# Two-layer hybrid trunk in split fp32: a new home and an earlier place for the weight sums of the mixers' output product, and an earlier place in DVE's queue for the third operand's split in the block products

## The chip, the cores and the metric

The kernel runs on one core of a Trainium2 chip. The metric is the time of one execution on the device in microseconds (us). The numbers of the time before are the median and the extremes of three runs; one further execution was taken by the hardware profiler, and every row of a view below is from that one. Engines are named as the profile names them: PE (matmul; PEld is its weight load), DVE (vector), ACT (scalar), POOL (GpSimd, here a queue of DMAs), SP (another queue of DMAs).

## The reference, cut to what matters

512 positions of width 1024 go through two layers in float32. Each layer is feed-forward, mixer, feed-forward:

```
for l in range(2):
    x = x + 0.5 * swiglu(rmsnorm(x, ln_ffn1[l]), w_ffn1_gu[l], w_ffn1_down[l])
    h = rmsnorm(x, ln_mix[l])
    u_pool, q, k, v, gate_logits = split(h @ w_in[l])
    a = pool_mixer(u_pool, pool_w[l], pool_scale[l]) @ w_pool_branch[l]
    b = swa_sink_attention(rope(norm(q)), rope(norm(k)), v, sinks[l]) @ w_attn_branch[l]
    g_pool, g_attn = split(sigmoid(gate_logits))
    x = x + (g_pool * a + g_attn * b) @ w_out[l]
    x = x + 0.5 * swiglu(rmsnorm(x, ln_ffn2[l]), w_ffn2_gu[l], w_ffn2_down[l])

swiglu(h, w_gu, w_down): g, u = split(h @ w_gu); return (silu(g) * u) @ w_down     # 1024 -> 2 x 2816 -> 1024
```

## The kernel before, in words

**Split products.** Every float32 operand is written as a rounded high part and a low part (the rest). ACT writes the high part with a cast (`wh<-raw`, `op<-fb`), and DVE writes the low part with a subtraction (`wl<-raw,wh`, `op<-fb,op`). A product is three matmuls: high by high, high by low, low by high.

**Block products.** Most large products are done in seven block products in place of eight, in the order of `ORDER` (line 27): a11, s1, s2, a12, s3, s4, a22. Each name stands for a weight block and an operand block; those of s1 to s4 are sums or differences of others. `strassen` (line 568) runs them. Each block product has two weight tiles, c = 0 and 1, and for each tile two column halves q = 0 and 1. After c = 0 it calls `W.prep()`, and after c = 1 the step of that block (`steps[kind]`, which takes the result out of PSUM) and then `W.prep()` again. Work that other engines are to do beside the matmuls hangs in the table `mid`: an entry `(kind, c, q)` is called when those matmuls have been written, so it stands in each engine's queue at that point. Results sit in three PSUM accumulators: a11, s2, s3 and a22 share one (A), s1 and s4 one (C), a12 has the third (D). A block that starts on an accumulator waits until the last result has been taken out of it.

**One queue for each engine.** The class `Engines` keeps every engine's instructions in the order in which the program writes them. An instruction that waits holds up all that stands behind it on its engine.

**The weights' pipeline** (class `Weights`, lines 184 to 326). `plan` lists all weight tiles in order of use. `load` brings tiles from HBM into 7 buffers (`raw`). SP issues the load, and where a block is a sum of two matrices, POOL issues a second DMA that adds the other matrix into the same buffer. A buffer is free once its `uses` are 0. `prep` keeps the high parts 4 tiles ahead of PE and the low parts 3 tiles ahead. The weights of s2 and s4 are sums of tiles that are there already; `add_up` writes them with DVE (`sums<-raw`) into `W.sums`. While `W.sums` is `None`, `add_up` stops at the first such tile, and the raw tiles that go into it keep their use.

**Feed-forward** (`ffn`, line 603). The 2816 hidden columns are worked in column groups, 512 or 384 wide at a time (`block`), and after two such blocks `down` (line 810) multiplies them by the down weights with a block product of its own. Each feed-forward has three downs: one with 384 columns (weight tiles of 1024 and 512 columns) and two with 512. The last one (`final`) is followed by the next norm, whose operands are already made beside it: `feeds` (line 558) writes PE transposes of x at fixed places of s3, s4 and a22, some into accumulator D. In `down` the operand of s3 is `f["b"]`; `high("s3", ...)` is called at `("s2", 0, 1)`, `low("s3")` in the step `s2`, after the `add` that takes the result of s2 into x. A block's result goes to two places of x in most cases: one by DVE (`add`), the other by an ACT copy into a buffer (`aside`) and a DMA on POOL that adds the copy into x (`gathered`).

**Mixer** (`mix`, line 922). After q, k, v, u and the gates, the loop over m (line 1241) runs eight branch products with the weights `br`, whose operands include the tiles `ah` and `al`; the last one, m = 7, writes into the PSUM tile `sc`. The output product with `w_out` follows as a block product. Its operand blocks are quarters of `ze`, made by DVE (`less`), and their split parts live in three places: `place[0]` for a11, a12 and a22, `place[1]` for s1 and s3, `place[2]` for s2 and s4. The first two operands are split in the loop itself (`beside`, at m = 4 to 7). `W.sums` is given its buffers after the loop, in the home of `al`. The step of a11 copies the result into `aside[0]` (`copied(0, ...)`, profile name `zo<-mm`), `gathered(0, 0, 0)` at `("s1", 1, 0)` adds it into x (`x<-zo` on POOL), and the step of s2 copies into the same `aside[0]` again, so that copy waits for the DMA.

Of the kernel before, what the change touches and what calls it, by code (L numbers as in the profile page):

```python
# [10 lines left out]
F32 = mybir.dt.float32  # L11
F32R = mybir.dt.float32r
# [7 lines left out]
P = 128  # L20
L = 2
S = 512
D = 1024
KT = D // P
FF = 2816
HT = S // 2
# [14 lines left out]
CH = 1024  # L41
# [78 lines left out]
def trunk(ctx, tc, x0, xT, consts, vecs, rows, w_g4, w_g3, w_d8, w_d6, w_qkv, w_u, w_pool, w_gate, w_br, w_out, out):  # L120
# [3 lines left out]
    wh_, wl_, xl = pool("wh", HI, side="left"), pool("wl", LO, side="left"), pool("xl", 1, side="left")  # L124
# [203 lines left out]
    W = Weights()  # L328
# [274 lines left out]
    def ffn(ctx, nm, nxt, last):  # L603
# [3 lines left out]
        sums = ctx.enter_context(tc.tile_pool(name="sums", bufs=2, reuse_waits="tile"))  # L607
# [14 lines left out]
        f, ops, turns = {}, {}, []  # L622
# [65 lines left out]
        def high(name, src, n):  # L688

            ops[name] = op.tile([P, 2, 2, S], F32R, name="op", tag=f"op{AT[name]}")  # L690
            hi, lo = (ops[name][:, i, :, :n] for i in range(2))
            nc.scalar.copy(out=hi, in_=src)
            ops[name, "low"] = lambda: nc.vector.tensor_tensor(
                out=lo, in0=src, in1=hi.bitcast(F32), op=ALU.subtract
            )

        def low(name):
            ops.pop((name, "low"))()
# [111 lines left out]
        def down(n, final):  # L810
# [3 lines left out]
            def add(t, d, c):  # L814
                def go(pt):
                    y = x[:, 2 * t:2 * t + 2, d * S:(d + 1) * S]
                    nc.vector.scalar_tensor_tensor(out=y, in0=pt, scalar=c, in1=y, op0=ALU.mult, op1=ALU.add)
                return go
# [13 lines left out]
            def aside():  # L832
                t, d, c, pt, half = pend_x[0]
                nc.scalar.activation(out=half, in_=pt, func=AF.Copy, scale=c)
# [14 lines left out]

            def s2(pt):  # L850
                add(1, 0, 0.5)(pt)
                low("s3")

            def a12(pt):
                add(0, 0, 0.5)(pt)
# [13 lines left out]
            def a22(pt):  # L869
# [7 lines left out]
            mid = {  # L877
                ("a11", 1, 0): lambda: low("s2"), ("s1", 0, 0): aside, ("s1", 0, 1): lambda: [low("a12"), gathered()],
                ("s2", 0, 1): lambda: [high("s3", f["b"], n), aside()],
                ("s2", 1, 0): gathered, ("a12", 0, 1): lambda: high("s4", f["c"], n),  # L880
                ("s3", 0, 0): lambda: ops.pop("t4")(), ("s3", 1, 0): lambda: high("a22", f["a"], n),
                ("s4", 0, 0): lambda: low("a22"),
            }
# [38 lines left out]
    def mix(ctx, l, nm, nxt):  # L922
        ap = ctx.enter_context(tc.tile_pool(name="ap", bufs=1, reuse_waits="tile"))
        ah, al = (ap.tile([P, 4, S], F32R, name=n) for n in ("ah", "al"))
        rp = ctx.enter_context(tc.tile_pool(name="rp", bufs=1, reuse_waits="tile"))
        mp = ctx.enter_context(tc.tile_pool(name="mp", bufs=1, reuse_waits="tile"))
# [4 lines left out]
        for i in range(3):  # L931
            n = order_.index(i)
# [20 lines left out]
        qkv = mp.tile([P, 5, S], F32, name="qkv")  # L953
# [261 lines left out]
        a, b, c, d = y[0][0], y[0][1], y[1][1], y[1][0]  # L1215
        place, ops = [None] * 3, {}

        def high(name, src):
            t = ops[name] = place[AT[name]]
            hi, lo = (t[:, :, i, :] for i in range(2))  # L1220
            nc.scalar.copy(out=hi, in_=src)
            ops[name, "low"] = lambda: nc.vector.tensor_tensor(
                out=lo, in0=src, in1=hi.bitcast(F32), op=ALU.subtract
            )

        def low(name):
            ops.pop((name, "low"))()
# [13 lines left out]
        for m in range(KT):  # L1241
            w = W.take("br")
            pts = (mm(), mm()) if m + 1 < KT else (wide[:, 0, :], wide[:, 1, :])
            for i, acts in enumerate((
                [part_of(k, slice(0, S)) for k in range(4)], [(ah[:, k, :], al[:, k, :]) for k in range(4)]
            )):
                gemm(pts[i], pairs(w, acts, 4 * i))
            zm = z[2 * m:2 * m + 2]
            for i in range(2):
                nc.scalar.activation(out=zm[i], in_=zm[i], func=AF.Sigmoid)  # L1250
            if m == 4:
                place[0] = rp.tile([P, 4, 2, HT], F32R, name="op0", tag="zo0")
                place[1] = mp.tile([P, 4, 2, HT], F32R, name="op1", tag="qkv")
            if m in beside:
                beside[m]()
            for i in range(2):
                nc.vector.tensor_tensor(out=zm[i], in0=pts[i], in1=zm[i], op=ALU.mult)
            nc.vector.tensor_tensor(out=zm[0], in0=zm[0], in1=zm[1], op=ALU.add)
            W.prep()
# [2 lines left out]
        three = [pf.tile([P, 2, S], F32, name=f"mm{i}") for i in range(3)]  # L1262
        turn = pf.tile([P, 2, S], F32, name="pt")
        roles = [three[i] for i in order_]
        place[2] = ap.tile([P, 4, 2, HT], F32R, name="op2", tag="ah")
        pair = ap.tile([P, 2, CH], F32, name="sums", tag="al")
        W.sums = Parts([pair[:, i, :] for i in range(2)])
        aside = [zo[1][:, 2 * i:2 * i + 2, :] for i in range(2)]

        def region(t, d):  # L1270
# [14 lines left out]
        def gathered(i, t, d):  # L1285
            return lambda: nc.gpsimd.dma_start(out=region(t, d), in_=aside[i], accum_op=ALU.add)
# [8 lines left out]

        def s2(pt):
            copied(0, pt, 1.0)
            low("s3")

        def a12(pt):  # L1300
            add(0, 0, pt)
# [12 lines left out]
        def a22(pt):  # L1314
# [8 lines left out]
        high("s2", a)  # L1323
        mid = {
            ("a11", 1, 0): lambda: low("s2"),
            ("s1", 0, 1): lambda: low("a12"), ("s1", 1, 0): gathered(0, 0, 0), ("s2", 1, 0): gathered(1, 1, 1),
            ("a12", 0, 0): gathered(0, 1, 0),
            ("a12", 0, 1): lambda: high("s4", c), ("s3", 0, 0): lambda: less(a, a, d, -1.0),
            ("s3", 1, 0): lambda: high("a22", a), ("s4", 0, 0): lambda: low("a22"),
# [126 lines left out]
```

## Time and profile before

| what | value |
|---|---|
| median of three runs (lowest, highest) | 1857.6 us (1857.4, 1858.55) |
| the profiled execution's own time | 1857.56 us |
| its span, first to last instruction | 1855.8 us |
| busy share of the span: PE, PEld, DVE, ACT, POOL | 99%, 83%, 78%, 57%, 9% |
| granted PE clock | 1.0 throughout |
| HBM read, mean over the span | 160 GB/s |
| costliest groups: `wl<-raw,wh` on DVE, `wh<-raw` on ACT | 509.3 us, 438.4 us |

A row of the timeline has the start, the time, the engine, the line (always L97, since a helper records everything), the operation, output and inputs by name, and how many were merged; in square brackets stands the idle time of that engine just before it, and what ended that. An end on PE is modelled: matmuls overlap, and one that follows another starts about 0.23 us after it although each is shown with 0.39 us. Idle time in brackets is counted from the modelled end, so the distance between two starts, less 0.23 us, says how much was really lost. A DVE or ACT row shows a little more than the distance between two starts as well (1.22 us for a 128x1024 subtraction, of which one can start every 1.14 us).

### The profile page before, as it was taken

To read this page: it belongs to the slowest core of one execution; us is meant where nothing else is said; L and a number is where in the kernel's file an instruction comes from. 1 tells how busy PE (TensorE), PEld (TensorE's weight loads), DVE (VectorE), ACT (ScalarE), POOL (GpSimd) and SP (SyncE) were. 2 spreads that over 40 slices of the span, in tenths; PEclk is the share of its full clock that TensorE was granted. 3 is DMA by queue.
4 is the path that set the end of the run, shared out by engine and by line. 5 is a ranking of instruction groups with operands and counts; after the bars stand their busy time and mean duration, and the time that the engine had idled before them with its cause. 6 is when DMAs were issued, how large, how long until landed. Compare 5 with 4: busy or idle time off the path is not lost.

```text
span 1855.8 us, 24041 instructions
## 1 busy us (share of the span) xinstructions
PE 1840.7 (99%) x8880; PEld 1548.0 (83%) x8880; DVE 1452.7 (78%) x1825; ACT 1051.4 (57%) x1533; POOL 165.7 (9%) x190
## 2 busy tenths in 40 slices
PE   9999999999999999999999999999999999999999
PEld 9988888887787889988878898888877878899887
DVE  8878878677568987887898878786675689788877
ACT  6655555645447655555675555565554477546554
POOL 0110101000001011110100111110000011101000
PEclk9999999999999999999999999999999999999999
DMA  8877867422247667787767768773222378777864
GB/s 255 210 227 193 216 170 192 132 80 71 82 109 192 193 180 186 191 223 192 195 169 205 169 182 232 199 186 108 91 69 83 100 193 216 178 187 179 244 182 125
DMA packets 97462, 314.85 MB, mean 170 GB/s; under 512 B 10528, under 2 KB 10784, under 8 KB 97344
## 3 DMA queue, kind: packets, MB, share of 16 engines
q1 hardware_dynamic: 67680, 225.57, 35.8%
q0 software_dynamic: 29520, 87.71, 27.5%
q8 instruction: 70, 1.15, 0.2%
q14 instruction: 48, 0.39, 0.1%
q10 hardware_dynamic: 144, 0.03, 0.0%
HBM read 295.44 MB, written 2.10 MB: 160 GB/s over the span
## 4 chain that ended last, share of the span: by engine, by line
PE 84%; DVE 7%; ACT 6%; DMA 2%; issue 1%; POOL 0%; DVEq 0%; ACTq 0%; POOLq 0%; SPq 0%
PE mm L97 76%; PE sc L97 3%; PE pt L97 3%; ACT wh L97 2%; DVE wl L97 2%; DVE sums L97 1%; DVE x L97 1%; DMA x<-zo 1%; ACT sq L97 1%; PE pt_pv L97 1%; ACT xg L97 1%; ACT more L97 0%; DVE more L97 0%; PE pt_tp L97 0%; ACT xgh L97 0%
## 5 line engine op out<-in xcount | busy, mean ns | idle before, releaser
L97 ACT CAST wh<-raw 128x1024 fp32r<-128x1024 f32 (+3 forms) x447 | 438.4, 989 | 285.4 <-PE mm L97 156.4
L97 DVE TENSOR_TENSOR wl<-raw,wh 128x1024 fp32r<-128x1024 f32 (+3 forms) x447 | 509.3, 1146 | 97.3 <-PE mm L97 59.6
L97 PE MATMUL mm<-wh,op 128*128 128x512 f32 x1456 | 464.2, 394 | 0.4 <-ACT zo L97 0.4
L97 PE MATMUL mm<-wh,more 128*128 128x512 f32 (+1 forms) x1104 | 334.0, 373 | 0.0
L97 PEld LDWEIGHTS mm<-wh,op 128*128 128x128 f32 x1456 | 273.2, 188 | 57.6 <-DVE op L97 1.6
L97 PE MATMUL mm<-wh,xgh 128*128 128x512 f32 (+2 forms) x840 | 312.5, 372 | 0.9 <-ACT xg L97 0.8
L97 PE MATMUL mm<-wh,xgl 128*128 128x512 f32 (+2 forms) x840 | 309.5, 368 | 0.0
L97 PE MATMUL mm<-wl,xgh 128*128 128x512 f32 (+2 forms) x840 | 309.4, 368 | 0.0
L97 PE MATMUL mm<-wl,op 128*128 128x512 f32 x728 | 284.0, 390 | 1.6 <-DVE wl L97 1.6
L97 PEld LDWEIGHTS mm<-wh,more 128*128 128x128 f32 x1104 | 205.2, 188 | 29.8
L97 PE MATMUL mm<-wl,more 128*128 128x512 f32 (+1 forms) x552 | 205.9, 373 | 1.2 <-DVE wl L97 1.2
L97 DVE TENSOR_TENSOR wl<-sums,wh 128x1024 fp32r<-128x1024 f32 (+2 forms) x148 | 168.7, 1140 | 44.7 <-ACT wh L97 29.4
L97 ACT CAST wh<-sums 128x1024 fp32r<-128x1024 f32 (+2 forms) x148 | 144.1, 984 | 86.8 <-DVE sums L97 43.7
L97 PEld LDWEIGHTS mm<-wh,xgh 128*128 128x128 f32 x840 | 157.9, 188 | 23.2 <-ACT xg L97 2.1
L97 PEld LDWEIGHTS mm<-wh,xgl 128*128 128x128 f32 x840 | 157.9, 188 | 21.5
L97 PEld LDWEIGHTS mm<-wl,xgh 128*128 128x128 f32 x840 | 158.1, 188 | 21.0 <-DVE wl L97 0.3
L97 PEld LDWEIGHTS mm<-wl,op 128*128 128x128 f32 x728 | 136.9, 188 | 30.1 <-DVE wl L97 3.3
L97 POOL DMA_DIRECT2D raw<-in_w_g x92 | 78.6, 855 | 717.5 <-DMA raw<-in_w_g 266.0
L97 PE MATMUL mm<-xgh,wh 128*128 128x512 f32 x320 | 129.2, 404 | 0.0
L97 PE MATMUL mm<-xgl,wh 128*128 128x512 f32 x320 | 125.3, 391 | 0.5 <-DVE xgl L97 0.5
L97 PE MATMUL mm<-xgh,wl 128*128 128x512 f32 x320 | 125.2, 391 | 0.0
L97 PEld LDWEIGHTS mm<-wl,more 128*128 128x128 f32 x552 | 103.6, 188 | 17.2 <-DVE wl L97 2.4
(252 smaller groups left out, 2252.8 us busy)
## 6 DMA issues: line engine op xcount, KB each, us to landing
raw<-in_w_g SPq DMA_DIRECT2D x160, 512.0 KB, 5.2
raw<-in_w_d SPq DMA_DIRECT2D x100, 512.0 KB, 4.4
raw<-in_w_g POOLq DMA_DIRECT2D x64, 512.0 KB, 6.1
raw<-in_w_g SPq DMA_DIRECT2D x77, 384.0 KB, 4.8
raw<-in_w_d POOLq DMA_DIRECT2D x40, 512.0 KB, 5.7
raw<-in_w_gate SPq DMA_DIRECT2D x32, 512.0 KB, 3.3
raw<-in_w_g POOLq DMA_DIRECT2D x28, 384.0 KB, 6.1
raw<-in_w_out SPq DMA_DIRECT2D x20, 512.0 KB, 3.6
```

What stands on the lines that cost most here:

```text
L97: return lambda *args, **kw: self.tc.keep_in_program_order(call(*args, **kw))
```

## The change

Four things are done. (1) In the loop over m, at m = 4, `W.sums` is opened, in the home of q, k and v, whose tile is no longer read then; `prep` can thus add up the weights of s2 within the loop. (2) The operand of s1 moves from that home to the home of the norm's low part (`xgl`), also no longer read. (3) After the loop, `place[1]` (now for s3 alone) and `place[2]` take the homes of `al` and `ah`. (4) In `down` and in the mixer's output product, `low("s3")` moves from the step `s2` to the entry `("s2", 1, 0)` of `mid`, that is, from behind the taking out of s2's result to half a weight tile before the end of s2's matmuls. What is computed stays the same, and no engine's count of instructions changes.

```
             def s2(pt):
                 add(1, 0, 0.5)(pt)
-                low("s3")
...
-                ("s2", 1, 0): gathered, ("a12", 0, 1): lambda: high("s4", f["c"], n),
+                ("s2", 1, 0): lambda: [low("s3"), gathered()], ("a12", 0, 1): lambda: high("s4", f["c"], n),
...
             if m == 4:
                 place[0] = rp.tile([P, 4, 2, HT], F32R, name="op0", tag="zo0")
-                place[1] = mp.tile([P, 4, 2, HT], F32R, name="op1", tag="qkv")
+                one = xl.tile([P, KT * S], F32R, name="op1", tag="xgl")[:, :2 * CH]
+                place[1] = one.rearrange("p (k i t) -> p k i t", i=2, t=HT)
+                four = mp.tile([P, 5, S], F32, name="sums", tag="qkv")[:, :4, :]
+                W.sums = Parts([four[:, 2 * i:2 * i + 2, :].rearrange("p i t -> p (i t)") for i in range(2)])
...
-        place[2] = ap.tile([P, 4, 2, HT], F32R, name="op2", tag="ah")
-        pair = ap.tile([P, 2, CH], F32, name="sums", tag="al")
-        W.sums = Parts([pair[:, i, :] for i in range(2)])
+        place[1:] = [ap.tile([P, 4, 2, HT], F32R, name=n, tag=n) for n in ("al", "ah")]
...
         def s2(pt):
             copied(0, pt, 1.0)
-            low("s3")
...
-            ("s1", 0, 1): lambda: low("a12"), ("s1", 1, 0): gathered(0, 0, 0), ("s2", 1, 0): gathered(1, 1, 1),
+            ("s1", 0, 1): lambda: low("a12"), ("s1", 1, 0): gathered(0, 0, 0), ("s2", 1, 0): lambda: [low("s3"), gathered(1, 1, 1)()],
```

How this moves the instructions is seen at three places. The first is DVE's queue in the down with 384 columns, around the end of s2; `op<-fb,op` is the low part of s3's operand, `x<-mm` takes out the result of s2, and `wl` and `sums` are weight tiles.

```order
 L97 TENSOR_TENSOR wl<-raw,wh 128x1024
 L97 TENSOR_TENSOR wl<-raw,wh 128x512
+L97 TENSOR_TENSOR op<-fb,op 128x2x384
 L97 SCALAR_TENSOR_TENSOR x<-mm_136,x 128x2x512
-L97 TENSOR_TENSOR op<-fb,op 128x2x384
 L97 TENSOR_TENSOR wl<-raw,wh 128x1024
 L97 TENSOR_TENSOR sums<-sums,raw 128x1024
```

The subtraction stands ahead of the taking out in place of behind it; nothing else moves, and the downs with 512 columns show the same.

The second is DVE's queue at the end of the mixer's loop (the first layer's), before the change. The rows begin at the end of m = 6: `op_4607` is the low part of s1's operand, the rows with `sc` take out m = 7, the `ze<-ze` after them makes the operand of s2, `op_4730` is its low part, and `sums<-raw` the two weight sums of s2.

```order
L97 TENSOR_TENSOR wl<-raw,wh 128x1024
L97 TENSOR_TENSOR op_4607<-ze,op_4607 128x4x256
L97 TENSOR_TENSOR ze<-sc,ze 128x512
L97 TENSOR_TENSOR zo_2993<-sc,zo_2993 128x512
L97 TENSOR_TENSOR ze<-ze,zo_2993 128x512
L97 TENSOR_TENSOR wl<-raw,wh 128x1024
L97 SCALAR_TENSOR_TENSOR ze<-ze 128x4x256
L97 TENSOR_TENSOR wl<-raw,wh 128x1024
L97 TENSOR_TENSOR sums<-raw 128x1024 x2
L97 TENSOR_TENSOR op_4730<-ze,op_4730 128x4x256
L97 TENSOR_TENSOR wl<-sums,wh 128x1024
```

And the same place in the changed kernel, where `ah` is now the name of the home of s2's operand:

```order
L97 TENSOR_TENSOR wl<-raw,wh 128x1024
L97 TENSOR_TENSOR sums<-raw 128x1024 x2
L97 TENSOR_TENSOR op_4607<-ze,op_4607 128x4x256
L97 TENSOR_TENSOR ze<-sc,ze 128x512
L97 TENSOR_TENSOR zo_2993<-sc,zo_2993 128x512
L97 TENSOR_TENSOR ze<-ze,zo_2993 128x512
L97 TENSOR_TENSOR wl<-raw,wh 128x1024
L97 SCALAR_TENSOR_TENSOR ze<-ze 128x4x256
L97 TENSOR_TENSOR wl<-raw,wh 128x1024
L97 TENSOR_TENSOR ah<-ze,ah 128x4x256
L97 TENSOR_TENSOR wl<-sums,wh 128x1024
```

The two sums stand seven instructions earlier, ahead of m = 7's results. ACT's queue has the same order as before here and in the rest of the output product, and so have DVE's later rows.

The third is SP's queue, with the semaphores that each load waits on: the last three loads of `w_out` and the two after them, before the change and then after it. `DMASW7` and `DMASW0` are the adding DMAs on POOL that filled the two tiles of s1, `DMAHW4` and `DMAHW5` the loads that filled those of a11; a load that waits on one of them takes that buffer.

```order
L97 DMA raw<-in_w_out 128x1024 [waits DMASW7_49,DVE_49,Activation_49]
L97 DMA raw<-in_w_out 128x1024 [waits DMAHW4_49,DMAHW2_49]
L97 DMA raw<-in_w_out 128x1024 [waits DMAHW5_49,DMAHW3_49,DVE_49]
L97 DMA raw<-in_w_g 128x1024 [waits DMASW0_49,Activation_49]
L97 DMA raw<-in_w_g 128x1024 [waits DMASW1_49,DVE_49]
```

```order
L97 DMA raw<-in_w_out 128x1024 [waits DMAHW4_49,DVE_49,Activation_49]
L97 DMA raw<-in_w_out 128x1024 [waits DMAHW2_49,DMAHW5_49,DVE_49,Activation_49]
L97 DMA raw<-in_w_out 128x1024 [waits DMASW7_49,DMAHW3_49,DVE_49,Activation_49]
L97 DMA raw<-in_w_g 128x1024 [waits DMASW0_49,DVE_49]
L97 DMA raw<-in_w_g 128x1024 [waits DMASW1_49,DVE_49]
```

The loads keep their order; the buffers they take change. The eighth load of `w_out` takes a buffer of a11 in place of one of s1. The order on POOL is the same in both kernels: the four adding DMAs of `w_out`, then the three `x<-zo`.

## The prediction

> **What bounds the kernel now.** I read the page first, then the waits of PE, then the timeline around each of them.
>
> ```profile
> PE 1840.7 (99%) x8880; PEld 1548.0 (83%) x8880; DVE 1452.7 (78%) x1825; ACT 1051.4 (57%) x1533; POOL 165.7 (9%) x190
> ...
> PE mm L97 <- DVE x L97: 4.0, 7, 1.4
> PE mm L97 <- DVE wl L97: 2.8, 7, 0.4
> PE mm L97 <- ACT xg L97: 0.8, 3, 0.3
> ```
>
> PE runs 99% of the span, so the change can win only what PE loses in waits. The table gives them by their last cause. They are few, and nearly all end with DVE: seven on `x` (a result taken out before PE may transpose x or reuse the accumulator) and seven on `wl` (a low weight part). DVE is busy 78% and is not the bound on average; it is late only where a queue of subtractions stands in front of the one that PE needs. The timeline says where.
>
> In the down with 384 columns (layer 1, second feed-forward; four of these in the program):
>
> ```profile
> 792.42 0.69 DVE L97 TENSOR_TENSOR wl<-raw,wh 128x512 fp32r<-128x512 f32 x1 [1.07 <-ACT u L97]
> 793.95 1.23 DVE L97 SCALAR_TENSOR_TENSOR x<-mm,x 128x1024 f32<-128x1024 f32 x1 [0.84 <-PE mm L97]
> 795.09 0.95 DVE L97 TENSOR_TENSOR op<-fb,op 128x768 fp32r<-128x768 f32 x1
> ...
> 801.44 1.22 DVE L97 TENSOR_TENSOR wl<-sums,wh 128x1024 fp32r<-128x1024 f32 x1
> ...
> 790.44 0.84 ACT L97 CAST op<-fb 128x768 fp32r<-128x768 f32 x1
> ...
> 801.69 0.61 PE L97 MATMUL mm<-wh,op 128*128 128x512 f32 x2
> 802.71 0.50 PE L97 MATMUL mm<-wl,op 128*128 128x512 f32 x1 [0.41 <-DVE wl L97]
> ...
> 806.92 0.39 PE L97 MATMUL mm<-wl,op 128*128 128x512 f32 x1
> 807.31 0.73 PE L97 MATMUL mm<-wh,op 128*128 128x512 f32 x2
> ```
>
> DVE waits 0.84 us for the end of s2, takes its result out (793.95), then splits s3's operand (795.09), and has no idle time from there to 801.44, the low weight for s4. PE wants that at 802.1 and starts at 802.71. Two matmuls take 0.61 us together and one 0.39, so starts are 0.22 to 0.23 us apart. From 801.69 to 802.71 are 1.02 us for two starts: 0.57 lost, and 0.11 more because the first matmul after the wait shows 0.50 us in place of 0.39. At 806.92 to 807.31 another 0.16 goes (a22's low operand, again from DVE's queue), with the same 0.11. That makes 0.95 us per such down.
>
> In the last down of a feed-forward (layer 0, first one; three are followed by a norm):
>
> ```profile
> 313.53 1.23 DVE L97 TENSOR_TENSOR wl<-raw,wh 128x1024 fp32r<-128x1024 f32 x1 [1.50 <-PE mm L97]
> 316.42 1.23 DVE L97 SCALAR_TENSOR_TENSOR x<-mm,x 128x1024 f32<-128x1024 f32 x1 [1.67 <-PE mm L97]
> 317.56 1.22 DVE L97 TENSOR_TENSOR op<-fb,op 128x1024 fp32r<-128x1024 f32 x1
> ...
> 323.24 1.22 DVE L97 SCALAR_TENSOR_TENSOR x<-mm,x 128x1024 f32<-128x1024 f32 x1
> ...
> 311.98 1.04 ACT L97 CAST op<-fb 128x1024 fp32r<-128x1024 f32 x1
> ...
> 337.94 0.63 PE L97 MATMUL mm<-cst,x 128*128 128x128 f32 x4 [0.25 <-DVE x L97]
> ...
> 342.27 0.50 PE L97 MATMUL mm<-xgl,wh 128*128 128x512 f32 x1 [0.23 <-DVE xgl L97]
> ```
>
> The same picture with 1.67 us of idle time before s2's result. Here the backlog reaches x (323.24 is a12's result), the transposes for the next norm (0.25 us idle, which by the rule above is 0.41 lost) and the next stage's first operand (0.23, so 0.39, and 0.11 after it).
>
> In the mixers' output product (layer 0):
>
> ```profile
> 553.83 1.22 DVE L97 TENSOR_TENSOR op<-ze,op 128x1024 fp32r<-128x1024 f32 x1
> 556.80 0.69 DVE L97 TENSOR_TENSOR ze<-sc,ze 128x512 f32<-128x512 f32 x1 [1.75 <-PE sc L97]
> 562.13 2.35 DVE L97 TENSOR_TENSOR sums<-raw 128x1024 f32<-128x1024 f32 x2
> ...
> 573.03 1.22 DVE L97 TENSOR_TENSOR op<-ze,op 128x1024 fp32r<-128x1024 f32 x1
> ...
> 579.77 1.23 DVE L97 TENSOR_TENSOR wl<-raw,wh 128x1024 fp32r<-128x1024 f32 x1 [3.25 <-ACT wh L97]
> ...
> 582.05 1.22 DVE L97 SCALAR_TENSOR_TENSOR x<-mm,x 128x1024 f32<-128x1024 f32 x1
> ...
> 563.46 1.05 ACT L97 CAST wh<-sums 128x1024 fp32r<-128x1024 f32 x1 [1.24 <-DVE sums L97]
> 564.42 1.02 ACT L97 ACTIVATE zo<-mm 128x1024 f32<-128x1024 f32 x1
> ...
> 577.78 1.02 ACT L97 ACTIVATE zo<-mm 128x1024 f32<-128x1024 f32 x1 [3.99 <-DMA x<-zo]
> ...
> 563.41 1.43 SPq L97 DMA_DIRECT2D raw<-in_w_out  x3
> ...
> 567.89 0.84 POOL L97 DMA_DIRECT2D raw<-in_w_out  x1 [20.10 <-DMA raw<-in_w_out]
> 568.43 1.53 POOL L97 DMA_DIRECT2D x<-zo  x1
> 573.41 1.18 POOL L97 DMA_DIRECT2D x<-zo  x1 [3.45 <-ACT zo L97]
> ...
> 578.86 0.50 PE L97 MATMUL mm<-wh,op 128*128 128x512 f32 x1 [0.41 <-ACT zo L97]
> ...
> 583.32 0.66 PE L97 MATMUL mm<-cst,x 128*128 128x128 f32 x4 [1.41 <-DVE x L97]
> ...
> 596.76 0.63 PE L97 MATMUL mm<-cst,x 128*128 128x128 f32 x4 [0.43 <-DVE x L97]
> ...
> 618.84 0.50 PE L97 MATMUL mm<-wh,xgh 128*128 128x512 f32 x1 [0.26 <-ACT xg L97]
> ```
>
> Read backwards: PE waits 1.41 us for a12's result (DVE, 582.05). DVE had stood 3.25 us for an ACT cast behind the copy at 577.78, and that copy had stood 3.99 us for the DMA `x<-zo`, since both use `aside[0]`. The DMA left POOL at 568.43, though its copy was done at 565.4 (564.42 and 1.02): ahead of it POOL stood 20.10 us for the eighth load of `w_out`, which SP issued at 563.41, when the first of the `sums` at 562.13 had freed a buffer. The weight sums thus hold up a DMA of x, and three waits later PE.
>
> **The change part by part.**
>
> *The split of s3 in the down.* One subtraction, with no DMA and no new instruction, moves from behind the taking out to ahead of it. It needs s3's high part, cast by ACT at 790.44 for 0.84 us (done 791.3) and at 311.98 for 1.04 us (done 313.0). DVE is free for it at 793.1 (792.42 and 0.69) and 314.8, so the cast is 1.7 us early. Its cost of 0.95 us falls into 0.84 us of idle time and that of 1.22 us into 1.67. What stood behind it comes 0.85 us and 1.14 us earlier. Behind it on DVE stand s2's `x<-mm` and the weights of s3 and a12; nobody new waits. POOL's `gathered` stands after it in program order only, as its own wait is on ACT and PE.
>
> With 384 columns, 801.44 becomes 800.6, its end 801.8, ahead of the 802.1 at which PE wants it; a22's operand is then late by at most 0.1. I take 0.9 us of the 0.95, times four downs: 3.6 us (2.7 if only the first wait goes, 0.68 each; 3.8 at most). With 512 columns and a norm behind, a12's result moves from 323.24 to 322.1. The wait at 337.94 goes (0.41), and the one at 342.27 for most of its 0.50, together with shorter late starts that no idle column marks; the bound is the 1.14 us by which the queue moves. I take 1.0 us, times three: 3.0 us (1.2 to 3.4). The other five downs show no wait and give nothing.
>
> *The sums of s2 in the mixer.* Two subtract-like additions, 1.14 us each, move to 553.83, ahead of s1's low operand, which then ends at 557.4, and s1 starts on PE near 562. The idle 1.75 us before 556.80 takes most of them; 0.5 us runs over and delays s2's operand. Its part on ACT starts 0.5 us later, but `wh<-sums` behind it loses its wait of 1.24, so the copy at 564.42 comes 0.8 us earlier and ends at 564.6. The sums now need only loads that landed long before and a home that nobody reads, so no wait is added. The eighth load leaves SP when the first sum is done, near 555, in place of 563.41, its adding DMA on POOL is issued near 560 in place of 567.89, and POOL is idle when the copy ends: `x<-zo` leaves at 564.7, 3.7 us earlier. If it takes as long as now (568.43 to 577.78, 9.3 us) it has landed at 574.0. The copy, the cast and DVE's 579.77 follow 3.8 us earlier, and a12's result is then bound by PE's own end of a12 at 578.5, not 582.05: 3.5 us earlier. That is before PE's transposes need it (581.0).
>
> *The homes.* s1's operand, s3's operand and the sums go to tiles whose last readers ended before; no instruction is added. s3's operand no longer overwrites s1's, which costs and gains nothing here, as its cast waits for `ze`.
>
> What is late next: after a12's result the chain runs DVE, ACT, DVE to the next norm's operands, all of it at most 3.5 us earlier. PE loses there, with 0.16 for each idle time and 0.11 after three of them: 0.41, 1.41, 0.43, 0.26, and one on `wl` of 0.4 from the table, 4.0 us in all. I take 3.4, the shift less a little (2.2, the first two alone; 4.0 at most).
>
> The mixer of layer 1:
>
> ```profile
> 1499.97 1.03 ACT L97 ACTIVATE zo<-mm 128x1024 f32<-128x1024 f32 x1 [2.90 <-DMA x<-zo]
> ...
> 1504.24 1.22 DVE L97 SCALAR_TENSOR_TENSOR x<-mm,x 128x1024 f32<-128x1024 f32 x1
> ...
> 1505.52 0.66 PE L97 MATMUL mm<-cst,x 128*128 128x128 f32 x4 [1.05 <-DVE x L97]
> ```
>
> ACT fell idle here at 1497.07 and there at 573.79, so the two mixers are 923.28 us apart; the earliest a12 result is 578.5 + 923.3 = 1501.8, and the shift 2.4 us, because the DMA landed earlier (wait of 2.90, not 3.99). PE loses 1.05 and 0.16 at first, and about 3.0 with the later ones, which are like those of layer 0. I take 2.4 (1.2 to 3.0).
>
> [...]
>
> The sum: 3.6 + 3.0 + 3.4 + 2.4 = 12.4 us. The profiled execution took 1857.56 us (span 1855.8), the same as the median of 1857.6. Forecast: 1857.6 − 12.4 = 1845.2 us. A difference of 0.2%, 3.7 us, is about what a measurement of this kernel can tell from none.
>
> **The rivals.** *Only the first waits go.* Behind each lies the next queue: in the norm's chain ACT has its own backlog and may not move with DVE. Then the ends are 2.7 + 1.2 + 2.2 + 1.2 = 7.3 us: 1850.3. For it: the chain alternates between two engines. Against: both were late from the same DMA, or the same DVE queue.
>
> [...]
>
> *It does not do what it says.* `x<-zo` lands when it did, since its 9.3 us may stretch, and the queue of DVE is refilled by casts that wait for PE: 1857.6. Against: 20.10 us of POOL's wait depend on one buffer, and DVE's idle time is there in all downs.
>
> *Slower: ACT's cast in front of DVE.* The moved split now stands ahead of s2's `x<-mm` and of the weights of s3, and waits for ACT. If the cast of `op<-fb` ended later than DVE's idle time does, all of DVE's queue would stand. Now it ends at 313.0, and the point from which it decides is 316.4 less 1.2, near 315.2, so 2.2 us of delay. A cast 5 us late would cost 2.8 us in each of the seven downs that are short of DVE, 19.6 us, against 5.8 won in the mixers: 1871. Against it: nothing is added in front of that cast.
>
> **How the numbers follow.** Likeliest, as worked out: 0.71. Only the first waits: 0.15. The port: 0.04. Nothing: 0.05. Slower: 0.05. The range reaches from all upper bounds (3.8 + 3.4 + 4.0 + 3.0 = 14.2, so 1843.4) to a little past the first rival, 1851. Faster by over 0.2% is the first three, 0.90; within it 0.05; slower 0.05.
>
> **What would show it.** In the profile after: no PE wait on `wl` within the downs (seven become three or fewer), PE's wait on `x` under 1 us in all, DVE's `op<-fb` right before `x<-mm` with its idle time nearly gone; POOL's wait for the eighth load ending near 560, `x<-zo` near 564.7, ACT's wait for it under 1.5 us. I am wrong if the waits on PE keep their sum of about 10 us, if PE waits for something new at s3 or s1, or if `x<-zo` still lands after 577.

## The result, and the profile after

The changed kernel takes 1845.59 us (median of six runs, 1844.91 to 1845.92), the kernel before 1857.51 us (1857.3 to 1858.76): a ratio of 0.9934, with a 95% interval of 0.9921 to 0.9946, or 11.9 us won. The profiled execution took 1845.1 us, its span is 1843.3 us. The forecast was 1845.2 us.

The page's share of PE, and the waits of PE (waited for, us in total, times, longest), now:

```profile
PE 1835.9 (100%) x8880; PEld 1548.6 (84%) x8880; DVE 1453.9 (79%) x1825; ACT 1051.8 (57%) x1533; POOL 165.8 (9%) x190
...
PE cold L97 <- DVE warm_in L97: 1.1, 1, 1.1
PE mm L97 <- ACT xg L97: 0.8, 3, 0.3
PE pt_pv L97 <- ACT qkv L97: 0.5, 2, 0.3
PE pt_tp L97 <- DVE zo L97: 0.5, 2, 0.2
```

The seven waits on `x`, the seven on `wl`, and those on `xgl` and `zo` (7.7 us by their idle time) are gone, and no new one stands in their place. DVE does the same work (1453 us) in a shorter span.

PE runs the same 8880 matmuls in the same order in both kernels. So the start of the n-th matmul in the trace of the kernel before, less its start in the trace of the changed one, tells how much has been won up to it, and the steps of this difference tell where. In us:

| place | forecast | measured |
|---|---|---|
| four downs with 384 columns | 3.6 | 0.51 + 0.86 + 0.57 + 0.75 = 2.7 |
| three last downs before a norm | 3.0 | 1.13 + 1.13 + 1.11 = 3.4 |
| mixer of layer 0 | 3.4 | 3.5 |
| mixer of layer 1 | 2.4 | 2.4 |
| elsewhere (the program's start, small pieces) | 0 | 0.4 |
| sum | 12.4 | 12.4 (spans: 1855.8 − 1843.3 = 12.5) |

The output product of the first mixer after the change, on DVE, ACT, POOL and SP's queue. At this place the changed kernel runs 2.0 us earlier on the clock than the one before, so 2.0 is to be added to compare these starts with those of before:

```profile
551.79 2.35 DVE L97 TENSOR_TENSOR sums<-raw 128x1024 f32<-128x1024 f32 x2
576.45 1.22 DVE L97 SCALAR_TENSOR_TENSOR x<-mm,x 128x1024 f32<-128x1024 f32 x1 [0.53 <-PE mm L97]
...
568.89 1.02 ACT L97 ACTIVATE zo<-mm 128x1024 f32<-128x1024 f32 x1
571.06 1.03 ACT L97 ACTIVATE zo<-mm 128x1024 f32<-128x1024 f32 x1 [0.22 <-ACT wh L97]
...
553.08 1.47 SPq L97 DMA_DIRECT2D raw<-in_w_out  x2
557.25 0.84 POOL L97 DMA_DIRECT2D raw<-in_w_out  x1 [11.48 <-DVE ze L97]
562.78 1.20 POOL L97 DMA_DIRECT2D x<-zo  x1 [4.69 <-ACT zo L97]
```

The sums stand at 551.79, so SP issues the eighth load at 553.08 (the row merges it with the ninth) and POOL its adding DMA at 557.25 (553.8, 555.1 and 559.3 on the clock of before). `x<-zo` leaves at 562.78, which is 564.8 on that clock, as forecast. The copy that stood 3.99 us for it (571.06) has 0.22 us of idle time ahead of it, and DVE takes out a12's result after a wait for PE itself (576.45, 0.53): the chain over ACT and the DMA binds no more.

What was not forecast is how long that DMA takes. Its rows by tile, for that one transfer, in the kernel before and then in the changed one (durations in ns, then the time from issue to landing in us):

```profile
L97 POOL DMA_DIRECT2D x<-zo x1: 1534/1534/1534, 568.4 to 568.4; - x1
DMA to landing us min/median/max: 9.2/9.2/9.2
```

```profile
L97 POOL DMA_DIRECT2D x<-zo x1: 1199/1199/1199, 562.8 to 562.8; - x1
DMA to landing us min/median/max: 5.0/5.0/5.0
```

The same 512 KB took 9.2 us before and 5.0 us now. The busy time by stretches (busy of PE, PEld, DVE, ACT, POOL with instructions, then PE's clock, the DMA engines' share and GB/s), before and then after, says what ran beside it:

```profile
555.00:560.00 5.00, 5.00 (x24) 4.14 (x23) 3.21 (x6) 1.05 (x1) 0.00 (x0) 1.00 0.00 0
...
565.00:570.00 5.00, 5.00 (x24) 4.15 (x23) 4.41 (x5) 4.21 (x5) 2.07 (x2) 1.00 0.97 358
570.00:575.00 5.00, 5.00 (x24) 4.14 (x23) 5.00 (x5) 2.91 (x3) 1.18 (x1) 1.00 1.08 222
```

```profile
555.00:560.00 5.00, 5.00 (x24) 4.14 (x23) 4.96 (x7) 0.99 (x2) 0.84 (x1) 1.00 0.69 197
...
562.80:565.00 2.20, 2.20 (x12) 1.81 (x11) 0.81 (x2) 2.20 (x3) 1.18 (x1) 1.00 0.99 348
565.00:567.80 2.80, 2.80 (x14) 2.33 (x13) 2.80 (x3) 1.38 (x2) 0.00 (x0) 1.00 0.91 155
567.80:570.40 2.60, 2.60 (x13) 2.13 (x13) 2.60 (x4) 2.47 (x3) 0.00 (x0) 1.00 0.02 6
```

Before, the DMA engines stood still from 555 to 560 (share 0.00) and were full from 565 on (0.97, then 1.08), with the loads and `x<-zo` at once. Now the loads run in the time that was empty (0.69 from 555 to 560). `x<-zo` meets the last two of them, which landed at 563.79 and 565.05 (share 0.99, 348 GB/s), and then runs alone until it lands at 567.8 (0.91, 155 GB/s; 0.02 after that). So the transfer took 9.2 us beside other transfers from start to end, and 5.0 us beside the ends of two loads.

### The profile page after: what moved, and what is told of

The parts are those of the page before. It is cut to its first block, busy times and chain, and to the rows that moved or that the text cites. A ratio compares the mean times of both kernels' runs of the same rounds, so it can differ in the third digit from the quotient of the medians.

```text
span 1843.3 us, 24049 instructions
## 1 busy us (share of the span) xinstructions
PE 1835.9 (100%) x8880; PEld 1548.6 (84%) x8880; DVE 1453.9 (79%) x1825; ACT 1051.8 (57%) x1533; POOL 165.8 (9%) x190
## 3 DMA queue, kind: packets, MB, share of 16 engines
q8 instruction: 70, 1.15, 0.2%
## 4 chain that ended last, share of the span: by engine, by line
PE 94%; DVE 3%; ACT 2%; issue 0%; DMA 0%; SPq 0%; DVEq 0%; ACTq 0%
PE mm L97 86%; PE sc L97 3%; PE pt L97 3%; PE pt_pv L97 1%; DVE wl L97 1%; ACT wh L97 1%; DVE more L97 0%; PE pt_tp L97 0%; ACT s L97 0%; DVE sums L97 0%; DVE hss L97 0%; ACT xg L97 0%; DVE win L97 0%; DMA op<-in_xT 0%; ACT p L97 0%
## 5 line engine op out<-in xcount | busy, mean ns | idle before, releaser
L97 PE MATMUL mm<-wh,op 128*128 128x512 f32 x1360 | 433.0, 393 | 0.0
L97 PEld LDWEIGHTS mm<-wh,op 128*128 128x128 f32 x1360 | 255.0, 188 | 53.1 <-DVE op L97 1.4
L97 PE MATMUL mm<-wl,op 128*128 128x512 f32 x680 | 265.0, 390 | 0.0
L97 PEld LDWEIGHTS mm<-wl,op 128*128 128x128 f32 x680 | 127.8, 188 | 25.7 <-DVE wl L97 0.6
```

The source lines that it names most:

```text
L97: return lambda *args, **kw: self.tc.keep_in_program_order(call(*args, **kw))
```

## The experiments

They were run in four groups, each with runs of the kernel before beside them (medians 1857.8, 1858.2, 1857.6 and 1858.9 us, single times from 1856.6 to 1860.7). Each kernel is compared with the runs of its own group. Short names (e1 to e12) stand beside them, since the expectations use them; e1 to e4 ran in the first group, e3c, e5, e6 and e7 in the second, e11, e3d and e8 in the third. Where a gain or loss of a place is told, it is again the difference of the starts of the same matmuls.

**The two halves apart.** The first kernel (e1) is the one before with the split alone moved (in the mixer in the same way):

```
             def s2(pt):
                 add(1, 0, 0.5)(pt)
-                low("s3")
...
-                ("s2", 1, 0): gathered, ("a12", 0, 1): lambda: high("s4", f["c"], n),
+                ("s2", 1, 0): lambda: [low("s3"), gathered()], ("a12", 0, 1): lambda: high("s4", f["c"], n),
```

> The kernel before with only low("s3") moved, in the downs and in the mixer; homes and sums stay. By the two traces PE won 2.7 us in the four downs with 384 columns, 3.4 in the three before a norm and 0.2 in another one. If the two halves of the change are independent, this kernel keeps these 6.3 us and nothing in the mixers: about 1851.3 us, with the mixers' waits of PE on DVE x (1.4 and 1.05 us) as before. Rival, that the split also helps in the mixers or only works together with the sums: below 1849, or above 1853.

Measured: 1853.48 us, 0.9973 (0.9963 to 0.9983), 4.3 us won where 6.3 were expected, and the median lies past the 1853 that was named for the rival. In the profiled execution the last downs won 1.15, 1.12 and 1.15 us, as in the whole change, and the second and third of the downs with 384 columns 0.75 and 0.86. The first and fourth lost 1.1 and 0.3 us, since DVE stood 1.54 and 1.11 us there for a DMA of x, `x<-p`, so these four won 0.2 us together, not 2.7. That DMA is looked at below, with the first down of e8. This kernel's times spread (1850.8 to 1854.4). The second kernel (e2) is the changed one with both splits put back:

```
             def s2(pt):
                 add(1, 0, 0.5)(pt)
+                low("s3")
```

> The changed kernel with low("s3") put back in both places; new homes and early sums stay. Independent halves: the mixers' 3.5 + 2.4 = 5.9 us are won, the downs' are not: about 1851.7 us, and seven PE waits on wl or x remain in the downs. Rival, that the mixers need the split too: less than 4 us won, above 1853.5.

Measured: 1851.44 us, 0.9966 (0.9954 to 0.9978), 6.3 us won; the mixers 3.53 and 2.40 us, the downs nothing, with five waits on `wl` left. So the mixers owe nothing to the split. That the downs owe nothing to the sums is not shown: in the trace of the split alone the downs with 384 columns won less than in the whole change.

**What of the split wins.** The changed kernel with a second subtraction in the old place (e4):

```
             def s2(pt):
                 add(1, 0, 0.5)(pt)
+                nc.vector.tensor_tensor(out=wide("r0")[:, :, :n], in0=f["b"],
+                    in1=ops["s3"][:, 0, :, :n].bitcast(F32), op=ALU.subtract)
```

> The changed kernel with a second subtraction of the same size in the old place of the split, behind the taking out of s2 in each down; its result goes to a tile that nobody reads. The split itself stays early. My theory (what counts is the length of DVE's queue behind x<-mm): the 6.3 us of the downs are lost again, about 1851.9 us, with PE waiting on wl at the four downs with 384 columns. Rival (what counts is that s3's operand is ready earlier): nothing is lost, 1845.6 us.

Measured: 1852.04 us, 0.9968 (0.9956 to 0.9981). Against the kernel before, the mixers won 3.53 and 2.40 us and each of the seven downs 0.00 or, for the last, −0.34. The early operand is worth nothing in itself; with DVE's queue behind `x<-mm` as long as before, all that the split had won is gone.

**When the cast is late** (the prediction's slower rival). Four extra ACT copies ahead of the cast of s3's high part, in the changed kernel (e6) and in the one before (e7):

```
-                ("s2", 0, 1): lambda: [high("s3", f["b"], n), aside()],
+                ("s2", 0, 1): lambda: [extra(4), high("s3", f["b"], n), aside()],
...
+            def extra(count):
+                for _ in range(count):
+                    nc.scalar.copy(out=wide("r0")[:, :, :n], in_=f["b"])
```

> The changed kernel with four extra ACT copies of fb (about 0.92 us each at 512 columns, 0.74 at 384) ahead of the cast of s3's high part in each down; their result is read by nobody. They make the cast late by 3.7 and 3.0 us, past the point (1.3 us late at 512 columns) from which the prediction's slower rival decides: the moved split must hold up x<-mm and all behind it, near 1.3 us in each down before a norm and 2 to 3 us in each with 384 columns. About 1845.6 + 4 + 10 = 1860 us; to be compared with the next kernel. If the split's place does not matter when its cast is late, this kernel stays 11.9 us below the next one.

> The kernel before with the same four extra ACT copies in each down. Its split stands behind x<-mm and runs in the hole that DVE has there while it waits for weights that ACT casts late, so the late cast itself costs nothing more; what it loses comes from the late weights alone: about 1857.6 + 8 = 1866 us. Exposed split: the lead of the changed kernel shrinks from 11.9 to about the mixers' 5.9 us. Not exposed: 11.9 stays.

Measured: 1858.87 us and 1861.71 us (1.0003, 0.9994 to 1.0012, and 1.0017, 1.0008 to 1.0027): the lead of 11.9 us shrinks to 2.8, though 5.9 was expected, and the second kernel is 4.3 us faster than the 1866 expected. By their spans the copies cost the changed kernel 13.8 us (1857.1 less 1843.3) and the other 3.6 (1859.4 less 1855.8). ACT and DVE of the changed kernel with the copies, in the last down of the first feed-forward, then the changed kernel's `x<-mm` without them, and then DVE of the kernel before with them:

```profile
312.71 4.29 ACT L97 COPY r<-fb 128x1024 f32<-128x1024 f32 x4
316.90 1.04 ACT L97 CAST op<-fb 128x1024 fp32r<-128x1024 f32 x1
...
317.98 1.22 DVE L97 TENSOR_TENSOR op<-fb,op 128x1024 fp32r<-128x1024 f32 x1 [2.49 <-ACT op L97]
319.12 1.22 DVE L97 SCALAR_TENSOR_TENSOR x<-mm,x 128x1024 f32<-128x1024 f32 x1
```

```profile
315.50 1.23 DVE L97 SCALAR_TENSOR_TENSOR x<-mm,x 128x1024 f32<-128x1024 f32 x1 [0.53 <-PE mm L97]
```

```profile
316.60 1.23 DVE L97 SCALAR_TENSOR_TENSOR x<-mm,x 128x1024 f32<-128x1024 f32 x1 [1.67 <-PE mm L97]
317.75 1.22 DVE L97 TENSOR_TENSOR op<-fb,op 128x1024 fp32r<-128x1024 f32 x1
319.29 1.23 DVE L97 TENSOR_TENSOR wl<-raw,wh 128x1024 fp32r<-128x1024 f32 x1 [0.33 <-ACT wh L97]
```

In the changed kernel DVE stands 2.49 us for the cast, and `x<-mm` behind it starts at 319.12; this execution runs 1.7 us behind the changed kernel at this place, where that row stands at 315.50, so the row is 1.9 us late, and PE lost 1.94 us in this down. In the other kernel the split runs behind `x<-mm` in time that DVE would have stood anyway (0.33 us are left). So the rival's mechanism is real, and costs more than the split brings; in the changed kernel the cast is early enough.

**What of the mixer wins.** The prediction's chain was: POOL stands for the eighth load, so `x<-zo` leaves late, so ACT's copy stands. First the copy alone is freed, with the kernel before and a third buffer for the copy of s2 (e3):

```
+        third = xl.tile([P, KT * S], F32, name="third", tag="xgl")[:, :CH]
+        aside.append(third.rearrange("p (i t) -> p i t", i=2))
...
-            copied(0, pt, 1.0)
+            copied(2, pt, 1.0)
...
-            ("a12", 0, 0): gathered(0, 1, 0),
+            ("a12", 0, 0): gathered(2, 1, 0),
```

> The kernel before with one edit: the copy in the mixer's step s2 goes to a third home (that of xgl) in place of aside[0], so it no longer waits for the DMA x<-zo. The sums stay after the loop, the eighth load stays late, x<-zo stays late. My theory (the DMA in front of ACT's copy is the whole cause): the copy starts near 574 in place of 577.78, and at least 5 of the mixers' 5.9 us are won: 1851.7 to 1852.6 us. Rival (what helps is that DVE has the two additions out of its way after the loop, 2.3 us): nothing or less than 1 us is won: 1856.6 to 1857.6.

Measured: 1855.01 us, 0.9983 (0.9974 to 0.9992), 2.8 us won, between what the theory and the rival gave. The copy and what came of its home:

```profile
573.55 1.02 ACT L97 ACTIVATE third<-mm 128x1024 f32<-128x1024 f32 x1
...
586.93 0.69 DVE L97 TENSOR_TENSOR xgl<-more,xgh 128x512 fp32r<-128x512 f32 x1 [2.60 <-ACT xgh L97]
```

The copy starts at 573.55 and stands for nothing, and in its trace the waits of PE that came first are gone (2.3 us won there in the first mixer and 1.2 in the second). Then DVE stands 2.60 us for the home itself: the cast named ended at 583.5, and what ends the wait is the DMA out of the third home, issued at 574.88 and landed at 586.5. PE lost 1.1 and 1.3 us again. The home was ill chosen: what the copy's stand cost is thus not yet told. One that nobody needs later is the quarter b of `ze` (e3d; its DMA is issued as two halves):

```
+        third = b.rearrange("p (i j) t -> p i j t", i=2)
...
-            copied(0, pt, 1.0)
             low("s3")
+            nc.scalar.activation(
+                out=third, in_=pt.rearrange("p i (j t) -> p i j t", t=HT), func=AF.Copy, scale=1.0
+            )
```

> The kernel before with the third home of e3 put elsewhere: the copy of s2 goes to the quarter b of ze, which nobody reads after s3's split, so that nothing waits for that home later; its x DMA is issued as two halves. Sums and loads late as before. If ACT's stand before that copy is what costs PE its first wait, and in e3 only the home gave the gain back (the next norm's xgl waited for the DMA out of it until 586.5), then at least 4 of the mixers' 5.9 us are won: 1851.9 to 1854 us. If the late loads hold up something else as well: above 1856 us.

Measured: 1852.76 us, 0.9972 (0.9961 to 0.9983), 4.9 us won. Its profiled execution took 3637.19 us, about twice the others, so its rows are not read here. The loads are as late as before in this kernel, and most of the 5.9 us is won: the copy's stand is what costs. The next kernel (e3c) is the one before with the cause that I gave for that stand taken away, POOL's order (`W.held` holds the eighth load's adding DMA back):

```
+        def first_gathered():
+            gathered(0, 0, 0)()
+            for go in W.held:
+                go()
+            W.held = None
...
+            ("s1", 0, 1): lambda: low("a12"), ("s1", 1, 0): first_gathered, ("s2", 1, 0): gathered(1, 1, 1),
```

> The kernel before with one swap in POOL's queue: the mixer's first x<-zo is issued ahead of the adding DMA of the eighth load of w_out, which it stood behind. Sums, homes, split and every other queue are as before. Theory (POOL's queue in front of x<-zo is the cause of what the mixers lose): x<-zo leaves at 565.4 in place of 568.4 and lands by 571, ACT's copy no longer stands for it, and 4.5 to 5.9 us are won: 1851.7 to 1853.1 us. Rival (DVE must have the two additions out of its way after the loop, 2.3 us in each mixer): less than 1.5 us won, above 1856.

Measured: 1856.96 us (one of its eleven executions took 2484 us), 0.9995 (0.9986 to 1.0004): no difference. This theory falls. POOL, that DMA's landing and ACT in this kernel:

```profile
566.11 1.19 POOL L97 DMA_DIRECT2D x<-zo  x1 [17.98 <-ACT zo L97]
...
575.95 1.03 ACT L97 ACTIVATE zo<-mm 128x1024 f32<-128x1024 f32 x1 [1.78 <-PE mm L97]
578.25 1.05 ACT L97 CAST wh<-raw 128x1024 fp32r<-128x1024 f32 x1 [1.27 <-DMA raw<-in_w_out]
```

```profile
DMA to landing us min/median/max: 9.7/9.7/9.7
```

`x<-zo` leaves at 566.1 (568.4 before) and takes 9.7 us, so it lands at 575.8 (577.7 before), and the copy still stands 1.78 us for it; PE, named in the row, is not what it waits for. Behind it ACT stands 1.27 us more, now for the eighth load itself, which carries weights of s3: its adding DMA, now behind `x<-zo`, landed at 578.2 in place of 575.2. So the swap only exchanged which of the two is late, and the theory left is that the loads come too late: beside them `x<-zo` took 9.2 us (before) and 9.7 us (here), and 5.0 us where it met only the ends of two (the changed kernel). So the next kernel (e11) is the changed one with its loads late (`held` keeps `load` from loading, `touch` puts a DVE write of one column ahead of the next three loads):

```
+            W.held = m >= 6
...
+        def released():
+            W.held, W.touch = False, 3
+            W.load()
...
+            ("a11", 1, 0): lambda: [low("s2"), released()],
```

> The changed kernel, with the sums early on DVE and all homes moved, but the three loads of w_out that take the freed buffers held back to about where they were before: DVE first writes one column of each buffer, behind s2's low operand (near 562 in place of 553). New theory, after the swap in POOL's queue won nothing: it is the loads that come late, 563 in place of 553. They run beside x<-zo (which then takes 9 us in place of 5) and land themselves only when ACT wants them. By it this kernel loses in the mixers what the change won there, 4 to 6 us: 1849.5 to 1852 us. Rival (the additions out of DVE's way after the loop): 1845.6 to 1846.5 us.

Measured: 1853.28 us, 0.9978 (0.9969 to 0.9986), 1.3 us above the range expected. Against the changed kernel, the mixers lost 3.80 and 2.50 us, all that they had won (3.5 and 2.4). The profiled execution took 1858.43 us, the longest of its eleven, since it lost another 6.2 us in the first down (below); at the place shown it is 6.6 us behind the changed kernel:

```profile
568.53 1.32 SPq L97 DMA_DIRECT2D raw<-in_w_out  x3
573.15 0.84 POOL L97 DMA_DIRECT2D raw<-in_w_out  x1 [20.79 <-DMA raw<-in_w_out]
573.69 1.53 POOL L97 DMA_DIRECT2D x<-zo  x1
...
582.57 1.02 ACT L97 ACTIVATE zo<-mm 128x1024 f32<-128x1024 f32 x1 [5.15 <-DMA x<-zo]
```

```profile
DMA to landing us min/median/max: 8.8/8.8/8.8
```

With the additions early and only the loads late, POOL stands again, `x<-zo` takes 8.8 us and the copy stands 5.15 us. That DVE has the additions out of its way wins nothing here. Last, the changed kernel with its loads early and only `x<-zo` late, behind the other one on POOL (e5):

```
-            ("s1", 1, 0): gathered(0, 0, 0), ("s2", 1, 0): lambda: [low("s3"), gathered(1, 1, 1)()],
+            ("s2", 1, 0): lambda: [low("s3"), gathered(1, 1, 1)(), gathered(0, 0, 0)()],
```

> The changed kernel, sums early and homes moved, but in the mixer the first x<-zo is issued by POOL behind the second one (of s1's result), so near 571.7 in place of 562.8, and lands near 581.5. Theory (the landing of this DMA sets the mixers): ACT's copy of s2 stands for it, 3.8 us longer than before the change did, PE stands at the start of s3, since that accumulator is not free, and both mixers lose more than before the change: 1857 to 1863 us. Rival (the additions out of DVE's way are what won): 1845.6 us.

Measured: 1863.42 us, 1.003 (1.0018 to 1.0042), slower than the kernel before. ACT's row, and PE's waits:

```profile
581.24 1.02 ACT L97 ACTIVATE zo<-mm 128x1024 f32<-128x1024 f32 x1 [9.72 <-DMA x<-zo]
```

```profile
PE mm L97 <- ACT zo L97: 10.9, 2, 5.6
```

The DMA landed at 581.1, near the 581.5 expected, and against the changed kernel the mixers lost 8.4 and 8.8 us. That is somewhat more than the landing explains, and is told in the last section.

**What is left, and a faster kernel.** The changed kernel's PE still waits three times for ACT `xg`, at the start of the feed-forwards after a norm. Two banks are swapped there (e8):

```
-                        mid["s1", 1, 0] = lambda: due(turn[:, 0, :])
-                        mid["s2", 0, 0] = lambda: due(roles[2][:, 0, :])
+                        mid["s1", 1, 0] = lambda: due(roles[2][:, 0, :])
+                        mid["s2", 0, 0] = lambda: due(turn[:, 0, :])
```

> The changed kernel with one more edit: at the start of the feed-forwards after a norm, the two late transposes of x swap their PSUM banks, so that the one into the bank that a12 uses is made in s1 and not in s2. In the profile of the changed kernel PE waits there three times for ACT xg, 0.42 us and 0.11 each by the distance between starts. If a12 waits only for that bank, all three go: 1.6 us, 1844.0 us. Rival (ACT's backlog reaches PE by another way): 1845.6 us.

Measured: 1844.79 us, 0.993 (0.9916 to 0.9944): 12.8 us below the kernel before of its group, where the changed kernel was 11.9 below. By the times alone that does not tell it apart from the changed kernel. In its trace the three waits are gone. But its profiled execution took 1849.18 us, the longest of its five, for another reason. DVE and PE in the first down of the program, and the stretch after the wait:

```profile
92.47 1.23 DVE L97 SCALAR_TENSOR_TENSOR x<-mm,x 128x1024 f32<-128x1024 f32 x1 [2.96 <-PE mm L97]
...
95.75 0.80 PE L97 MATMUL mm<-wl,op 128*128 128x512 f32 x1 [2.58 <-DVE wl L97]
96.34 1.06 PE L97 MATMUL mm<-wh,op 128*128 128x512 f32 x2
```

```profile
95.70:98.90 3.20, 3.15 (x8) 2.51 (x8) 2.25 (x3) 1.35 (x2) 0.87 (x1) 0.50 1.06 394
```

DVE stands 2.96 us, not for PE as the row says, which had long been done, but for the down's own DMA of x, `x<-p`: a12's result is added to the part of x that this DMA adds into, and the DMA landed at 92.4. POOL issues it behind an adding DMA of the next weights, as in the mixer. The same DMA is what DVE stood for in the first down of e1 (it landed at 91.6, and `x<-mm` started at 91.71) and of e11 (94.0 and 94.06). In the changed kernel's own trace it is there in small, in the third down with 384 columns:

```profile
1117.67 0.95 DVE L97 TENSOR_TENSOR op<-fb,op 128x768 fp32r<-128x768 f32 x1
1118.59 1.23 DVE L97 SCALAR_TENSOR_TENSOR x<-mm,x 128x1024 f32<-128x1024 f32 x1
1123.49 1.23 DVE L97 SCALAR_TENSOR_TENSOR x<-mm,x 128x1024 f32<-128x1024 f32 x1 [0.20 <-DMA x<-p]
...
1130.96 0.39 PE L97 MATMUL mm<-wl,op 128*128 128x512 f32 x1
1131.37 0.73 PE L97 MATMUL mm<-wh,op 128*128 128x512 f32 x2
```

The split fills DVE's idle time as forecast, but the next `x<-mm` stands 0.20 us for `x<-p` (0.27 in the first), and a22's operand comes 0.18 us late (1130.96 to 1131.37 is 0.41). So the last kernel (e12) has the swap of banks and issues `x<-p` first in those downs (the edit that collects the adding DMAs in `W.held` is as in e3c and not shown, nor is the swap again):

```
             def gathered():
...
                 nc.gpsimd.dma_start(out=x[:, 2 * t:2 * t + 2, d * S:(d + 1) * S], in_=half, accum_op=ALU.add)
+                for go in W.held or ():
+                    go()
+                W.held = None
 
             pend_x = []
+            W.held = []
```

> The changed kernel with the swap of banks of e8 and, in the eight downs that are not the last of a feed-forward, POOL's x<-p issued ahead of the adding DMA of the next weights, which it stands behind in the changed kernel (at 81.43 behind 80.89). There DVE's taking out of a12 waits for x<-p in two of the four downs with 384 columns (0.27 and 0.20 us), and for 3 to 4.5 us in the first down of two other runs. If POOL's queue is what makes x<-p late there, these waits go, in the first down above all, the four downs give back 0.3 to 1 us and the spread of the times shrinks: 1843.2 to 1844.3 us. Rival (as in the mixer, an x DMA that leaves earlier takes longer beside the loads, or the weights behind it come late): 1844.8 us as e8, or more.

Measured: 1843.39 us (1843.26 to 1844.45), 0.992 (0.9906 to 0.9933), 15.5 us below the kernel before of its group. The interval overlaps that of the changed kernel (0.9921 to 0.9946), so by the ratios alone it is not shown to be faster than that one; the traces show what follows. Its waits of PE (the one on `wh` stands at 5.3 us, in the program's start), and `x<-p` in the first down:

```profile
PE cold L97 <- DVE warm_in L97: 1.1, 1, 1.1
PE mm L97 <- ACT wh L97: 0.6, 1, 0.6
PE pt_pv L97 <- ACT qkv L97: 0.5, 2, 0.3
PE pt_tp L97 <- DVE zo L97: 0.5, 2, 0.2
```

```profile
L97 POOL DMA_DIRECT2D x<-p x1: 1199/1199/1199, 79.8 to 79.8; - x1
DMA to landing us min/median/max: 6.4/6.4/6.4
```

`x<-p` leaves at 79.8 in place of 81.4 and lands at 86.2 in place of 89.7, and no DVE row that takes out a result in the first down stands for it. Its span of 1841.6 us is 1.7 below that of the changed kernel: 0.8 in the four downs, 0.8 net at the three feed-forwards (each wins 0.53 and gives back about 0.25 in single starts of matmuls a few us later).

## Why the prediction was right, point by point

- *The split, 512 columns.* Right: 1.13, 1.13 and 1.11 us measured, nearly the whole 1.14 by which the queue moves, where 1.0 was taken. The extra subtraction showed that the queue's length is the cause.
- *The split, 384 columns.* The mechanism was right, the size off: 2.7 us, not 3.6, and 2.7 was the lower bound. The step that failed is "nobody new waits". In the first and third of these downs a12's `x<-mm` came earlier than `x<-p` had landed, and "a22's operand is then late by at most 0.1" became 0.16 and 0.18, with 0.11 after each. The second and fourth won 0.86 and 0.75.
- *The sums, what goes.* Right in place and size: 3.5 and 2.4 us for 3.4 and 2.4. In the changed kernel it is the early loads that win it: with the loads alone held back it was lost again. The wait they take away is the copy's; a home of its own for the copy took most of it away with the loads late (4.9 us won).
- *The sums, why.* Right that ACT's copy stood for `x<-zo` and that `x<-zo` came late because of the loads; wrong in two ways that did not show in the sum. "If it takes as long as now" did not hold (5.0 us, not 9.2). And that the weight sums "thus hold up a DMA of x" is not a matter of POOL's queue alone: with `x<-zo` ahead in that queue nothing was won, since it then ran beside the same loads (9.7 us), and the eighth load was late itself (its adding DMA landed at 578.2). That the DMA became nearly twice as fast added nothing to the sum, since PE's own end of a12 bound the chain already.
- *The homes.* Right: no operand waits for one. The third home of e3 shows what a badly chosen one costs.
- *What is late next.* Right for the mixers: PE's own end of a12 binds (0.53 us of DVE's idle time before 576.45). For the downs, x's DMA was not named.
- *The sum.* 12.4 us by the traces is the 12.4 forecast, and the medians say 11.9. That the two meet to a tenth is luck: the downs with 384 columns won 0.9 us less than forecast, and 0.4 more in the last downs and 0.4 in places priced at nothing made up for it.
- *The rivals.* Only the first waits go: fell, as later waits went with them. Nothing is won: fell, as POOL's wait for the eighth load ended at 557.25. The port, which had a chance of 0.04 (POOL's issue of `x<-zo` is held up beside DVE): the trace after does not show it; the second one (570.47) was issued in 1.18 us beside a subtraction of DVE (570.09 to 571.3), and the first (562.78), most of which fell into DVE's idle time, in 1.20. The late cast: real as a mechanism, but not met in the changed kernel, where DVE still has 0.53 us of idle time before `x<-mm` (315.50).

## What to carry to other kernels

A buffer freed late can cost more than the wait of whoever loads it: the load then runs in a crowded stretch (before, a DMA share of 0.97 and 1.08 from 565 to 575), and another DMA beside it took nearly twice its time (9.2 us for 5.0), so read the DMA share by stretches before blaming the order of a queue. Work moved into an engine's idle time wins what its queue is shortened by (here 1.11 to 1.13 us of 1.14), up to the next thing that the queue waits for; look for that thing, which here was a DMA of the result itself. And work moved ahead of an instruction must be ready early by more than its producer can slip.

## What was not expected of the hardware

After the wait of PE in the first down above (e8), the granted clock was 0.50 in the next 3.2 us, and matmuls of 512 columns started 0.43 us apart in place of 0.23 (96.34 for two, then 97.19): a wait of 2.6 us cost another 1.7 (the starts up to 99 us, less 0.23 each). In the late `x<-zo` (e5) PE waits twice, 10.9 us together and 5.6 us at the longest, and the mean granted clock of the profiled execution was 0.996, where the changed kernel's was 1.00. The mixers lost 6.3 us there beyond these waits (8.4 + 8.8 − 10.9). That the clock took most of it is an estimate from that mean: 0.4% of the span of 1861.6 us is 7.4 us, in which time within the waits may count too. The longest wait of PE between matmuls in the kernels before and after, 1.41 us (583.32 before), left the granted clock at 1.00 (584 to 588).

One and the same adding DMA of 512 KB into x, the first `x<-zo` of the mixer, took 5.0 us beside the ends of two loads (changed kernel) and 8.8 to 9.7 us beside the weights' loads (before, e11 and e3c); the one from the third home took 11.6 us.
